# The boundaries of a two-layer latent trunk in a fixed order: pinned tail products, statistics and rows, a Newton iteration spread over the norm, early weight loads

## The chip, the cores and the metric

The kernel runs on one core of a Trainium2 chip. Its time is the device time of one execution in microseconds, the median of several runs; lower is better. The engines that matter here are TensorE (PE in the profile; PEld is its weight load), VectorE (DVE), ScalarE (ACT), GpSimd (POOL) and SyncE (SP), which issues nearly all transfers.

## What is computed

The reference is a trunk of two layers over 256 latent tokens and 256 context tokens, each of 1024 features. Each layer has three sub-layers, each with a norm ahead of it and a gated residual behind it:

```python
def rmsnorm(x, g):
    y = x * lax.rsqrt(jnp.mean(x * x, axis=-1, keepdims=True) + NORM_EPS)
    return y * g
def modulate(h, shift, scale):
    return h * (1 + scale) + shift
def ffn_half_step(h, m, k, g, w_gate, w_up, w_down):
    shift, scale, gate = m[:, :, 3 * k], m[:, :, 3 * k + 1], m[:, :, 3 * k + 2]
    hn = modulate(rmsnorm(h, g), shift, scale)
    return h + 0.5 * gate * swiglu(hn, w_gate, w_up, w_down)
...
for i in range(DEPTH):                       # DEPTH = 2
    m_lat = adaln_params(c, mod_w[i], mod_b[i])       # 9 vectors of 1024
    m_ctx = adaln_params(c_ctx[None, :], mod_w[i], mod_b[i])
    lat, cx = ffn_half_step(lat, m_lat, 0, ...), ffn_half_step(cx, m_ctx, 0, ...)
    # i = 0: latent attention heads and S5 groups; i = 1: Hyena and RG-LRU channels
    lat, cx = lat + m_lat[5] * y_lat, cx + m_ctx[5] * y_ctx
    lat = ffn_half_step(lat, m_lat, 2, ...)
    if not last: cx = ffn_half_step(cx, m_ctx, 2, ...)
return rmsnorm(lat, final_norm)
```

The feed-forward width is 2816. All of it is float32.

## The kernel before

**Layout.** Features lie on the 128 partitions and tokens in the free dimension: a feature tile is 128 x 512, columns 0 to 255 context (`CTX`), 256 to 511 latent (`LAT`). The residual `res` stays in SBUF as eight such tiles.

**Products.** A float32 product is made of three passes (`mm3`, L149 to L151): high part of the weights with the high part of `x` (L149), high with low (L150), low with high (L151). `wload` fetches a block of weights into `raw` (four buffers, SyncE's queue), ScalarE casts it into the high part (L141), and a subtraction gives the low part (L142): on VectorE, but on GpSimd for the second and third block of each norm's front. The split weights `w` have four buffers.

**Sub-layers and boundaries.** The order is ffn(0,0), even mixer, ffn(0,2), ffn(1,0), odd mixer, ffn(1,2) on the latent half alone, final norm. At the end of a sub-layer `down` takes the first five feature tiles with both halves at once, and the last three, the *tail*, half by half: three context tiles (128x256), then three latent ones. `residual` (L394) adds each into `res`; `stat` squares it (L269, ScalarE) and adds it to the half's `acc` (L270). `rstd_stats` sums `acc` over the partitions (two products with one column, L236) and takes 1/sqrt by three Newton iterations on one-column tiles (L241 to L249: `rs_v`, `rs_a`, `rs_y`); `rstd_rows` spreads the result over the partitions by two products (L256). Then comes the *front* of the next sub-layer, `norm_proj`: `norm_tile` makes `nt` (L287, VectorE), the high part of `x` (L292, ScalarE) and the low part (L294, VectorE), and each tile of `x` goes at once into the products of three blocks, eight context tiles first, then eight latent ones. Statistics and rows of the latent half come near the end of the context tiles.

**Order.** A scheduler decides at build time in which order each engine's instructions stand. `high_priority(offset=SOON)` lets a group go ahead of others; `keep` (keep_in_program_order) pins an instruction behind the one pinned before it on its engine. Before, the Newton steps, norm steps, statistics and rows are pinned; the products of tail and front are not.

**Background jobs.** Two kinds of work are cut into steps that `tick` doles out between the products: `mod_job` computes the vectors of `adaln_params` by reductions on VectorE (L215, 128x1024, one for each condition and feature tile), and `s5_prepare` and `hyena_prepare` build the matrices of the mixers. In `s5_chunk` (eight passes) six rounds double a row of angles (L635), and `_wrap` (L451, L452) takes the nearest integer off after each.

**Pools.** SBUF is divided anew for each stage (`phase`). The first use of a new stage's tile waits for all users of the pools that were given back.

## Time and profile before

| | before |
|---|---|
| median of 3 runs | 1827.52 us (1824.61 to 1829.32) |
| span of the profiled execution | 1825.2 us |
| PE busy | 1742.0 us (95%), 9364 products |
| DVE busy | 1307.9 us (72%), 2582 instructions |
| ACT busy | 684.6 us (38%) |
| POOL busy | 37.0 us (2%), 57 instructions |
| chain that ended last | PE 83%, DVE 9%, DMA 3%, ACT 2% |

The busy time of an engine is a mean over stretches of different kind. In the 40 slices of the page PE stands at nine tenths or more nearly everywhere. Lower digits lie in the first slice, in the last and in five between.

### The profile page before, as it was taken

The numbers are of one execution on the slowest core, as the hardware profiler recorded it, in microseconds if no ns is written. First come the engines' busy times: TensorE is split into PE (matmuls) and PEld (weight loads), VectorE is DVE, ScalarE is ACT, GpSimd is POOL, SyncE is SP. The second block draws the span as 40 slices with busy tenths as digits, with TensorE's granted clock in tenths as the row PEclk, the third lists the DMA queues.
The fourth block names the chain that finished last, engine by engine and source line by source line (L and its number), as shares of the span: only waits on it lengthen the run. The fifth ranks groups of instructions, "written<-read, shape, count | busy, mean of one in ns | idle before, by whom it ended". The sixth has DMA issues, their size and how long they took to land.

```text
span 1825.2 us, 24880 instructions
## 1 busy us (share of the span) xinstructions
PE 1742.0 (95%) x9364; PEld 1456.1 (80%) x9364; DVE 1307.9 (72%) x2582; ACT 684.6 (38%) x1082; POOL 37.0 (2%) x57
## 2 busy tenths in 40 slices
PE   5999999997999998999999999999999989789997
PEld 3778777787877787778888888888888888589997
DVE  7999999898578667775666677766653476975555
ACT  4433333333345654222222233222122247554442
POOL 0000000001000000000000010000000000010000
PEclk9999999998998999999999999999999999889998
DMA  8466666652465452664554533554533225236562
GB/s 320 167 213 203 207 205 202 211 193 96 124 187 160 131 170 89 191 208 141 159 184 150 161 116 124 175 174 152 171 116 93 81 81 198 71 130 194 181 190 92
DMA packets 108057, 292.64 MB, mean 160 GB/s; under 512 B 21217, under 2 KB 36449, under 8 KB 107681
## 3 DMA queue, kind: packets, MB, share of 16 engines
q1 hardware_dynamic: 102368, 287.39, 49.2%
q10 hardware_dynamic: 4928, 2.10, 0.6%
q0 software_dynamic: 640, 1.57, 0.3%
q8 instruction: 73, 1.20, 0.3%
q14 instruction: 48, 0.39, 0.1%
HBM read 272.20 MB, written 18.28 MB: 159 GB/s over the span
## 4 chain that ended last, share of the span: by engine, by line
PE 83%; DVE 9%; DMA 3%; ACT 2%; issue 1%; SPq 1%; DVEq 0%; ACTq 0%
PE mm L149 26%; PE mm L150 26%; PE mm L151 26%; DVE w L142 1%; DMA raw<-in_wgu_dram 1%; DVE acc L270 1%; DVE rs_y L249 1%; ACT w L141 1%; DMA x<-d_g 1%; DMA h<-in_modw_dram 1%; DMA x<-d_v 0%; SPq L943 0%; DVE rs_a L247 0%; DVE nt L287 0%; DVE junk L215 0%
## 5 line engine op out<-in xcount | busy, mean ns | idle before, releaser
L150 PE MATMUL mm<-x,w 128*128 128x512 f32 (+1 forms) x1792 | 631.6, 355 | 3.3 <-DVE x L294 3.3
L151 PE MATMUL mm<-x,w 128*128 128x512 f32 (+1 forms) x1792 | 630.1, 354 | 0.0
L149 PE MATMUL mm<-x,w 128*128 128x512 f32 (+1 forms) x1792 | 613.9, 357 | 11.4 <-ACT x L292 9.9
L141 ACT CAST w<-raw 128x1024 fp32r<-128x1024 f32 (+2 forms) x328 | 332.5, 1018 | 532.8 <-issue 267.4
L142 DVE TENSOR_TENSOR w<-raw,w 128x1024 fp32r<-128x1024 f32 (+2 forms) x318 | 376.5, 1187 | 164.0 <-ACT w L141 163.3
L149 PEld LDWEIGHTS mm<-x,w 128*128 128x128 f32 x1792 | 334.9, 192 | 65.8 <-ACT x L292 10.9
L150 PEld LDWEIGHTS mm<-x,w 128*128 128x128 f32 x1792 | 343.4, 192 | 52.2 <-DVE x L294 4.3
L151 PEld LDWEIGHTS mm<-x,w 128*128 128x128 f32 x1792 | 343.1, 192 | 49.3 <-issue 1.8
L215 DVE CUSTOM_DVE_ANT_0 junk<-m,sc 128x1024 f32<-128x1024 f32 x256 | 312.4, 1220 | 2.2
L149 PE MATMUL mm<-h,w 128*128 128x512 f32 (+1 forms) x776 | 270.3, 351 | 0.0
L150 PE MATMUL mm<-h,w 128*128 128x512 f32 (+1 forms) x776 | 270.1, 349 | 0.0
L151 PE MATMUL mm<-h,w 128*128 128x512 f32 (+1 forms) x776 | 269.8, 349 | 0.0
L150 PEld LDWEIGHTS mm<-h,w 128*128 128x128 f32 x776 | 146.2, 188 | 21.2 <-issue 1.4
L149 PEld LDWEIGHTS mm<-h,w 128*128 128x128 f32 x776 | 145.9, 189 | 21.5 <-issue 1.1
L151 PEld LDWEIGHTS mm<-h,w 128*128 128x128 f32 x776 | 146.2, 188 | 20.3 <-issue 0.4
L394 DVE SCALAR_TENSOR_TENSOR res<-mm,mraw,res 128x256 f32<-128x256 f32 x192 | 86.1, 479 | 97.1 <-PE mm L151 96.6
L422 DVE TENSOR_TENSOR h<-h,mm 128x512 f32<-128x512 f32 (+1 forms) x88 | 54.6, 620 | 125.2 <-PE mm L151 108.5
L421 ACT ACTIVATE h<-mm 128x512 f32<-128x512 f32 (+1 forms) x88 | 47.9, 544 | 238.3 <-PE mm L151 238.2
L292 ACT ACTIVATE x<-nt,mraw 128x256 fp32r<-128x256 f32 x88 | 43.0, 506 | 75.3 <-DVE nt L287 75.2
L156 DVE TENSOR_TENSOR h<-h,h 128x512 fp32r<-128x512 f32 (+1 forms) x88 | 54.4, 618 | 0.0
L155 ACT CAST h<-h 128x512 fp32r<-128x512 f32 (+1 forms) x88 | 49.6, 564 | 9.1 <-DVE h L422 9.0
L269 ACT ACTIVATE sq<-res 128x256 f32<-128x256 f32 x84 | 33.3, 413 | 50.4 <-DVE res L394 38.5
(324 smaller groups left out, 1437.1 us busy)
## 6 DMA issues: line engine op xcount, KB each, us to landing
raw<-in_wgu_dram SPq DMA_DIRECT2D x176, 512.0 KB, 3.6
m<-in_modw_dram SPq DMA_DIRECT2D x130, 512.0 KB, 4.2
raw<-in_wd_dram SPq DMA_DIRECT2D x64, 512.0 KB, 3.7
raw<-in_wd_dram SPq DMA_DIRECT2D x32, 384.0 KB, 3.3
raw<-in_od_in_dram SPq DMA_DIRECT2D x20, 512.0 KB, 3.5
h<-in_modw_dram SPq DMA_DIRECT2D x12, 512.0 KB, 10.4
raw<-in_ev_in_dram SPq DMA_DIRECT2D x10, 512.0 KB, 3.8
d_mb<-mbt SPq DMA_DIRECT2D x16, 256.0 KB, 3.0
```

The source lines that it names most:

```text
L141: nc.scalar.copy(w[:, 0, :n], raw[:, :n])
L142: (nc.gpsimd if pool else nc.vector).tensor_sub(w[:, 1, :n], raw[:, :n], w[:, 0, :n])
L149: mm(ps, lhsT=wh, rhs=xh, start=first and i == 0, stop=False)
L150: mm(ps, lhsT=wh, rhs=xl, start=False, stop=False)
L151: r = mm(ps, lhsT=wl, rhs=xh, start=False, stop=last and i == n - 1)
L155: self.nc.scalar.copy(hi, src)
L156: self.nc.vector.tensor_sub(lo, src, hi)
L215: nc.vector.tensor_tensor_reduce(self.junk, w, self.sc[:, v, :], 1.0, 0.0, ALU.mult, ALU.add, raw[:, dt, v : v + 1])
L292: self.last_act = nc.scalar.activation(x[:, 0, c0:c1], y, AF.Identity, bias=b)
L394: self.nc.vector.scalar_tensor_tensor(r, ps[:, c0:c1], gate[:, i, VEC[h] : VEC[h] + 1], r, op0=ALU.mult, op1=ALU.add)
L421: nc.scalar.activation(s[:, 0, lo:hi], pg[:, lo:hi], AF.Silu)
L422: nc.vector.tensor_mul(s[:, 1, lo:hi], s[:, 0, lo:hi], pu[:, lo:hi])
```

## The change

The places where one sub-layer ends and the next begins are written out in a fixed order.
- `down` pins every tail product (`keep=True`). The statistics of the context half stand behind the fifth of the eight feature groups of the first latent tail tile, its row products behind the second latent tail tile. Before the tail, the next sub-layer's first block is loaded (`self.ready`).
- `norm_proj` takes that block, loads the second into tiles of the stage's own pools (`spare`: `x`, `y` or `h`, `g`) and the third into `w`, and pins all front products. The latent half's statistics start at the fourth context tile (`j == 3`), and Newton is given out in four quarters over the tiles 3 to 6; the row products follow ahead of the last context tile. The first two norm steps are not pinned.
- No subtraction of weights is left on GpSimd.
- `phase` makes its pools with `reuse_waits="tile"`: a tile waits only for the users of its own bytes.
- In `mod_job` the five vectors of layer 1 with m > 4 are computed for the latent condition alone (32 reductions fewer).
- In `s5_chunk` `_wrap` is called twice a pass, on wider ranges, instead of six times.

```diff
-            p = self.stage.enter_context(self.tc.tile_pool(name=self.uid(tag), bufs=bufs))
+            p = self.stage.enter_context(self.tc.tile_pool(name=self.uid(tag), bufs=bufs, reuse_waits="tile"))
...
-        (nc.gpsimd if pool else nc.vector).tensor_sub(w[:, 1, :n], raw[:, :n], w[:, 0, :n])
+        if tag is None:
+            w = self.wp.tile([P, 2, 1024], F32R, tag="w", name=self.uid("w"))
+            hi, lo = w[:, 0], w[:, 1]
+        else:
+            hi, lo = (self.slot(tag, [P, 1024], F32R) for _ in range(2))
+        nc.scalar.copy(hi[:, :n], raw[:, :n])
+        nc.vector.tensor_sub(lo[:, :n], raw[:, :n], hi[:, :n])
...
-                for v in range(2):
+                for v in range(1 if l and m > 4 else 2):
...
+        ws = [self.ready, self.wload(srcs[1], D, spare), self.wload(srcs[2], D)] if spare else None
...
+                low[j]()
+                if j == 3:
+                    self.st = self.rstd_steps([self.acc[halves[1]]], self.inv_d)
+                if 3 <= j < 7:
+                    next(self.st[2], None)
             for w, ps in zip(ws, pss):
-                self.mm3(ps[:, h[0] : h[1]], self.wparts(w, KT)[i : i + 1], self.parts(xs[i : i + 1], *h), i == 0, i == KT - 1)
+                self.mm3(ps[:, h[0] : h[1]], self.wparts(w, KT)[i : i + 1], self.parts(xs[i : i + 1], *h), i == 0, i == KT - 1, keep=True)
...
+        ws = [(i, self.wload(blocks(i), n * P), self.pm()) for i in range(KT - tail, KT)]
+        self.ready = self.wload(after, D)
+        for h in halves:
+            for m, (i, w, ps) in enumerate(ws):
+                for j in range(n):
+                    if h is halves[1] and (m, j) == (0, 5):
+                        with self.tc.high_priority(offset=SOON):
+                            st = self.stats(halves[0])
+                    self.mm3(
+                        ps[:, h[0] : h[1]], self.wparts(w, n)[j : j + 1], self.parts(xs[j : j + 1], *h), j == 0, j == n - 1, keep=True
+                    )
+                self.residual(i, ps, gate, h, last)
+                if h is halves[1] and m == 1:
                     with self.tc.high_priority(offset=SOON):
-                        self.rb[h] = self.rstd_rows(*self.stats(h))
+                        self.rb[halves[0]] = self.rstd_rows(*st)
...
-            n, tt = a[:, :, w : 2 * w], tm[:, : 8 * w].rearrange("p (g c) -> p g c", g=8)
-            e.tensor_add(n, a[:, :, :w], tn[:, g8].unsqueeze(2).to_broadcast([P, 8, w]))
-            self._wrap(e, n, tt)
+            e.tensor_add(a[:, :, w : 2 * w], a[:, :, :w], tn[:, g8].unsqueeze(2).to_broadcast([P, 8, w]))
+            if w in (4, 32):
+                x = a[:, :, 1 : 2 * w] if w == 4 else a[:, :, 8 : 2 * w]
+                self._wrap(e, x, tm[:, : 8 * x.shape[-1]].rearrange("p (g c) -> p g c", g=8))
```

**TensorE at the third boundary**, from ffn(0,2) to ffn(1,0). `mm_8848`, `mm_8854` and `mm_8860` are the three tail tiles, `acc_8674` is the context half's sum, `ps_8945` holds its statistics and rows, `x_9052` is the first tile of the norm, and `mm_9075` to `mm_9077` are the front's three blocks. Before:

```order
L149 MATMUL mm_8854<-h_8346,w_8851 128x256
L236 MATMUL ps_8945<-inv_d,acc_8674 128x1 x2
L150 MATMUL mm_8854<-h_8346,w_8851 128x256
...
L151 MATMUL mm_8860<-h_8632,w_8857 128x256
L256 MATMUL ps_8945<-ident,rs_y_8949 128x128 x2
L149 MATMUL mm_9075<-x_9052,w_9062 128x256
L149 MATMUL mm_9076<-x_9052,w_9067 128x256
L149 MATMUL mm_9077<-x_9052,w_9072 128x256
L150 MATMUL mm_9075<-x_9052,w_9062 128x256
```

The same place of the change; the tail tiles are now `mm_8786`, `mm_8792` and `mm_8798`, the second block lies in the spare tiles `h_8997` and `h_8998`, the third in `w_9003`:

```order
L155 MATMUL mm_8786<-h_8354,w_8783 128x256 x3
L253 MATMUL ps_8903<-inv_d,acc_8612 128x1 x2
L155 MATMUL mm_8786<-h_8428,w_8783 128x256 x3
...
L155 MATMUL mm_8792<-h_8570,w_8789 128x256 x3
L278 MATMUL ps_8903<-ident,rs_y_8907 128x128 x2
L155 MATMUL mm_8798<-h_8067,w_8795 128x256 x3
...
L155 MATMUL mm_9014<-x_9006,w_8801 128x256 x3
L155 MATMUL mm_9015<-x_9006,h_8997 128x256 x2
L155 MATMUL mm_9015<-x_9006,h_8998 128x256
L155 MATMUL mm_9016<-x_9006,w_9003 128x256 x3
L155 MATMUL mm_9014<-x_9007,w_8801 128x256 x3
```

The statistics moved from the second latent tail tile up into the first, the row products from behind the last latent tail tile to ahead of it (24 products follow them), and a tile of the front takes all its nine products in a row, block by block. The latent half's statistics now stand behind the front's third context tile, before behind the sixth.

**VectorE at the same place.** `w_9322` is the fourth block's low part, `w_9062` to `w_9072` the front's three. Before:

```order
L241 TENSOR_SCALAR rs_v_8948<-ps_8945 128x2
L270 TENSOR_TENSOR acc_8677<-acc_8677,sq_8993 128x256
L242 TENSOR_SCALAR rs_y_8949<-rs_v_8948 128x2
L243 TENSOR_SCALAR rs_v_8948<-rs_v_8948 128x2
...
L270 TENSOR_TENSOR acc_8677<-acc_8677,sq_9021 128x256
L394 SCALAR_TENSOR_TENSOR res<-mm_8860,mraw_8_6518,res 128x256
L287 SCALAR_TENSOR_TENSOR nt_9078<-res,mraw_1_7323,ps_8945 128x256
L287 SCALAR_TENSOR_TENSOR nt_9081<-res,mraw_1_7323,ps_8945 128x256
L142 TENSOR_TENSOR w_9322<-raw_9320,w_9322 128x1024
```

With the change; `w_9003` is the third block's low part, `w_9261` and `w_9303` are the fourth's and fifth's:

```order
L267 SCALAR_TENSOR_TENSOR rs_a_8908<-rs_y_8907,rs_v_8906 128x1
L149 TENSOR_TENSOR w_9003<-raw_9001,w_9003 128x1024
L267 SCALAR_TENSOR_TENSOR rs_a_8908<-rs_y_8907,rs_v_8906 128x1
...
L309 SCALAR_TENSOR_TENSOR nt_9020<-res,mraw_1_7261,ps_8903 128x256
L149 TENSOR_TENSOR w_9261<-raw_9259,w_9261 128x1024
L292 TENSOR_TENSOR acc_8615<-acc_8615,sq_8962 128x256
L316 SCALAR_TENSOR_TENSOR x_9006<-nt_9017,mraw_0_6885,x_9006 128x256
...
L429 SCALAR_TENSOR_TENSOR res<-mm_8798,mraw_8_6456,res 128x256
L149 TENSOR_TENSOR w_9303<-raw_9301,w_9303 128x1024
L316 SCALAR_TENSOR_TENSOR x_9008<-nt_9033,mraw_0_6885,x_9008 128x256
...
L309 SCALAR_TENSOR_TENSOR nt_9134<-res,mraw_1_7261,ps_9063 128x256
L316 SCALAR_TENSOR_TENSOR x_9013<-nt_9115,mraw_0_6885,x_9013 128x256
```

The third block's subtraction stands inside the context half's Newton steps, those of two more blocks among the first norm steps, and the first latent norm step (`nt_9134`, which reads the latent rows in `ps_9063`) ahead of the low part of the last context tile (`x_9013`).

**VectorE at the first boundary**, from ffn(0,0) to the even mixer. Before, reductions of the background job (L215, an ISA row each) and S5's angles (L635, L452) stand among the Newton steps:

```order
L635 TENSOR_TENSOR et_2602<-et_2602,sb_19_162 128x8x32
L247 SCALAR_TENSOR_TENSOR rs_a_3782<-rs_y_3781,rs_v_3780 128x1 x2
L270 TENSOR_TENSOR acc_3521<-acc_3521,sq_3853 128x256
L451 TENSOR_SCALAR tm_2385<-et_2602 128x256
L249 SCALAR_TENSOR_TENSOR rs_y_3781<-rs_a_3782,rs_y_3781 128x1 x2
L452 TENSOR_TENSOR et_2602<-et_2602,tm_2385 128x8x32
L215 ISA junk_625,mraw_7_2401<-m_2627,sc_624 128x1024
```

With the change the same Newton steps follow each other:

```order
L269 SCALAR_TENSOR_TENSOR rs_y_3737<-rs_a_3738,rs_y_3737 128x1
L267 SCALAR_TENSOR_TENSOR rs_a_3738<-rs_y_3737,rs_v_3736 128x1 x2
L269 SCALAR_TENSOR_TENSOR rs_y_3737<-rs_a_3738,rs_y_3737 128x1 x2
L267 SCALAR_TENSOR_TENSOR rs_a_3738<-rs_y_3737,rs_v_3736 128x1
L149 TENSOR_TENSOR w_3871<-raw_3869,w_3871 128x1024
```

All reductions and angles of this stage now stand ahead of the tail. The fifth boundary, from the odd mixer to ffn(1,2), keeps its order.

## Rows read from the trace of the kernel before

**Rows 1.** Windows: length, busy us (instructions) by engine, granted clock, DMA share, GB/s.

```profile
65.00:430.00 365.00, 361.61 (x1752) 291.36 (x1750) 335.28 (x679) 130.38 (x205) 5.76 (x11) 1.00 0.63 201
```

**Rows 2.** Timeline of PE, third boundary: start, us, instruction, [idle before it].

```profile
1063.58 0.29 PE L149 MATMUL mm<-h,w 128*128 128x256 f32 x1
...
1099.29 0.85 PE L149 MATMUL mm<-x,w 128*128 128x256 f32 x4 [0.32 <-ACT x L292]
```

**Rows 3.** Windows over the four boundaries, columns PE, PEld, DVE, ACT, POOL.

```profile
407.81:450.60 42.79, 32.61 (x250) 30.73 (x248) 36.95 (x106) 14.61 (x27) 4.83 (x2) 0.84 0.37 120
669.14:706.57 37.43, 32.22 (x235) 30.76 (x233) 24.78 (x71) 11.53 (x21) 4.74 (x2) 0.91 0.22 72
1063.58:1099.29 35.71, 31.09 (x233) 29.99 (x232) 23.46 (x68) 11.53 (x21) 4.75 (x2) 0.90 0.23 74
1443.92:1480.41 36.49, 31.47 (x233) 30.45 (x231) 23.45 (x66) 11.54 (x21) 4.75 (x2) 0.91 0.18 58
```

**Rows 4.** Timeline of PE inside the third boundary.

```profile
1076.30 0.50 PE L236 MATMUL ps<-inv_d,acc 128*128 128x1 f32 x4
1076.66 0.36 PE L150 MATMUL mm<-h,w 128*128 128x256 f32 x1
...
1081.14 0.28 PE L151 MATMUL mm<-h,w 128*128 128x256 f32 x1
...
1097.47 0.71 PE L256 MATMUL ps<-ident,rs_y 128*128 128x128 f32 x4 [0.50 <-DVE rs_y L249]
1097.99 0.38 PE L150 MATMUL mm<-x,w 128*128 128x256 f32 x1
```

**Rows 5.** Timeline of PE, second boundary: filter products.

```profile
703.24 0.64 PE L990 MATMUL ps<-y 33*64 33x256 f32 x2
```

**Rows 6.** Timeline of PE, first boundary: a group of S5 products.

```profile
408.98 0.43 PE L614 MATMUL ps<-gs,bank 128*32 128x128 f32 x8
```

**Rows 7.** Lines of PE, third boundary: busy us, mean ns, idle before and its releasers.

```profile
L149 PE MATMUL mm<-x,w 128*128 128x256 f32 x24 | 5.4, 343 | 1.1 <-ACT x L292 1.1
L256 PE MATMUL ps<-ident,rs_y 128*128 128x128 f32 x8 | 1.4, 301 | 2.5 <-DVE rs_y L249 2.5
```

**Rows 8.** Timeline of DVE, third boundary.

```profile
1076.92 2.24 DVE L270 TENSOR_TENSOR acc<-acc,sq 128x256 f32<-128x256 f32 x1
...
1079.74 2.43 DVE L249 SCALAR_TENSOR_TENSOR rs_y<-rs_a,rs_y 128x1 f32<-128x1 f32 x2
...
1084.94 1.22 DVE L142 TENSOR_TENSOR w<-raw,w 128x1024 fp32r<-128x1024 f32 x1
...
1086.80 0.48 DVE L287 SCALAR_TENSOR_TENSOR nt<-res,mraw,ps 128x256 f32<-128x256 f32 x1
1087.19 0.48 DVE L294 SCALAR_TENSOR_TENSOR x<-nt,mraw,x 128x256 fp32r<-128x256 f32 x1
...
1095.48 0.16 DVE L241 TENSOR_SCALAR rs_v<-ps 128x2 f32<-128x2 f32 x1 [3.87 <-PE ps L236]
...
1098.22 0.48 DVE L287 SCALAR_TENSOR_TENSOR nt<-res,mraw,ps 128x256 f32<-128x256 f32 x1 [0.28 <-PE ps L256]
```

**Rows 9.** Windows with TensorE's granted clock, columns as in rows 1.

```profile
622.00:626.00 4.00, 2.79 (x23) 1.87 (x24) 0.00 (x0) 3.58 (x6) 0.75 (x1) 1.00 0.65 168
1088.00:1090.00 2.00, 2.00 (x11) 2.00 (x11) 2.00 (x7) 1.34 (x3) 0.00 (x0) 0.50 0.49 199
```

**Rows 10.** Lines of DVE from 409.5 to 440 us, first boundary.

```profile
L215 DVE CUSTOM_DVE_ANT_0 junk<-m,sc 128x1024 f32<-128x1024 f32 x9 | 10.9, 1216 | 0.0
L635 DVE TENSOR_TENSOR et<-et,sb 128x16 f32<-128x16 f32 (+4 forms) x5 | 3.5, 696 | 0.0
```

**Rows 11.** Timeline of ACT, third boundary: a cast.

```profile
1075.30 1.05 ACT L141 CAST w<-raw 128x1024 fp32r<-128x1024 f32 x1 [1.88 <-PE mm L151]
```

**Rows 12.** Timeline of DVE, second boundary: first of the filter steps.

```profile
703.92 0.54 DVE L991 TENSOR_SCALAR y<-ps,y 64x256 f32<-64x256 f32 x1 [0.37 <-PE ps L990]
```

**Rows 13.** Source line 452, the subtraction of `_wrap`: ns min/median/max, times, forms.

```profile
L452 DVE TENSOR_TENSOR et<-et,tm x48: 165/206/427, 98.1 to 429.7; 128x8 f32<-128x8 f32 x8, 128x16 f32<-128x16 f32 x8, 128x32 f32<-128x32 f32 x8, 128x64 f32<-128x64 f32 x8
```

More of the change, by code (lines that the diff above doesn't have):

```diff
@@ L37 @@
 NPASS = 8
+EVEN, ODD = (7, 8, 4), (12, 13, 14)
 GPP = 4
@@ L229, in rstd_stats, with rstd_steps @@
     def rstd_stats(self, accs, inv):
+        rb, y, steps = self.rstd_steps(accs, inv)
+        for _ in steps:
+            pass
+        return rb, y
+    def rstd_steps(self, accs, inv):
         cols = [a[:, j : j + P] for a in accs for j in range(0, a.shape[-1], P)]
@@ L321, in norm_proj @@
             return xs, pss
-        ws = [self.wload(s, D, i > 0) for i, s in enumerate(srcs)]
         pss = [self.pm() for _ in srcs]
+        first = lambda: self.tc.high_priority(offset=SOON)
         if len(halves) == 1:
-            self.rb[halves[0]] = self.rstd_rows(*self.stats(halves[0]))
-        todo = [(n, h, i) for n, h in enumerate(halves) for i in range(KT)]
+            ws = [self.wload(s, D) for s in srcs]
+            h = halves[0]
+            self.rb[h] = self.rstd_rows(*self.stats(h))
+            tile = lambda i: self.norm_tile(l, k, i, h, xs[i])
+            with first():
+                low = tile(0)
+            for i in range(KT):
+                with first():
+                    nxt = tile(i + 1) if i + 1 < KT else None
+                    low()
+                low = nxt
+                for w, ps in zip(ws, pss):
+                    self.mm3(ps[:, h[0] : h[1]], self.wparts(w, KT)[i : i + 1], self.parts(xs[i : i + 1], *h), i == 0, i == KT - 1)
+            return xs, pss
+        todo = [(h, i) for h in halves for i in range(KT)]
         low = {}
@@ L362, in wparts, with down @@
     def wparts(self, w, n, m=P, o=0):
-        return [(w[:, 0, o + i * m : o + (i + 1) * m], w[:, 1, o + i * m : o + (i + 1) * m]) for i in range(n)]
-    def down(self, blocks, xs, gate, halves, last, n):
+        return [(w[0][:, o + i * m : o + (i + 1) * m], w[1][:, o + i * m : o + (i + 1) * m]) for i in range(n)]
+    def down(self, blocks, xs, gate, halves, last, n, after=None):
         lo, hi = halves[0][0], halves[-1][1]
@@ L377, in down @@
                 self.tick()
-        if tail:
-            ws = [(i, self.wload(blocks(i), n * P), self.pm()) for i in range(KT - tail, KT)]
-            for h in halves:
-                for i, w, ps in ws:
-                    self.mm3(ps[:, h[0] : h[1]], self.wparts(w, n), self.parts(xs, *h))
-                    self.residual(i, ps, gate, h, last)
-                if h is not halves[-1]:
+        if not tail:
+            return
+        ws = [(i, self.wload(blocks(i), n * P), self.pm()) for i in range(KT - tail, KT)]
[11 more added lines that the diff above has]
+                if h is halves[1] and m == 1:
                     with self.tc.high_priority(offset=SOON):
-                        self.rb[h] = self.rstd_rows(*self.stats(h))
+                        self.rb[halves[0]] = self.rstd_rows(*st)
     def stats(self, h):
@@ L398, in residual, with blocks, ffn @@
             self.stat(i, h)
-    def ffn(self, l, k, halves, lead=None):
+    def blocks(self, idx, n=3):
+        return [self.t["wgu"][idx, b // 2, b % 2] for b in range(n)]
+    def ffn(self, l, k, halves, after=None, spare=None, lead=None):
         nc, t = self.nc, self.t
@@ L405, in ffn @@
         wgu = t["wgu"][idx]
-        blocks = [wgu[f, g] for f in range(2) for g in range(2)]
-        xs, pss = self.norm_proj(l, k, halves, blocks if lead else blocks[:3], lead)
+        xs, pss = self.norm_proj(l, k, halves, self.blocks(idx, 4 if lead else 3), lead, spare if len(halves) > 1 else None)
         if lead is not None:
@@ L427, in ffn @@
             gate = self.need(l, 3 * k + 2)
-            self.down(lambda i: t["wd"][idx, i][:, f0 * P : f1 * P], hid, gate, halves, f1 == NF, f1 - f0)
+            self.down(lambda i: t["wd"][idx, i][:, f0 * P : f1 * P], hid, gate, halves, f1 == NF, f1 - f0, after)
     def proj(self, name, blk, xs, c0, c1):
@@ L659, in even_mixer @@
         blk = t["ev_in"]
-        xs, pss = self.norm_proj(0, 1, both, [blk[i] for i in (7, 8, 4)])
+        xs, pss = self.norm_proj(0, 1, both, [blk[i] for i in EVEN], spare="x")
         qn = self.const([P, 5], "qkvn", t["qkvn"])
@@ L1068, in odd_mixer @@
         both = [CTX, LAT]
-        xs, pss = self.norm_proj(1, 1, both, [t["od_in"][12 + i] for i in range(3)])
+        xs, pss = self.norm_proj(1, 1, both, [t["od_in"][i] for i in ODD], spare="g")
         pss.append(self.proj("od_in", 15, xs, 0, T2))
```

91 lines of the change are left out of this document (41 added, 50 removed).

## The prediction, made before the changed kernel ran

> **What bounds the kernel now.** I read the windows first. In the long feed-forward stretches TensorE never stops: in 65 to 430 us it is busy 361.6 of 365.0 us, although VectorE, the next engine, is busy 335.3 [rows 1]. No cut in another engine's work can shorten such a stretch. What is left to win lies where one sub-layer ends and the next begins, because there the norm stands between the last products and the first ones. So I measured those places in the timeline of TensorE: from the first product of the tail (three feature tiles taken half by half, 128x256) to the first latent product of the next sub-layer's front [rows 2]. Between them stand always the same 144 tail products and 72 context products of the front, two groups of statistics products and two of row products. Four such boundaries exist. Windows laid from the first to the last of these products give 42.8, 37.4, 35.7 and 36.5 us, in which TensorE is idle for 10.2, 5.2, 4.6 and 5.0 and is granted a mean clock of 0.84 to 0.91 [rows 3].
>
> The least that they can last comes from the timeline. 38 products from 1076.66 to 1081.14 give 4.48 / 37 = 0.121 us each; a group of statistics takes 1076.66 - 1076.30 = 0.36, a group of row products 1097.99 - 1097.47 = 0.52 [rows 4]. 216 x 0.121 + 2 x 0.36 + 2 x 0.52 = 27.9 us. So the third boundary loses 35.7 - 27.9 = 7.8 us and the fourth 8.6. In the second, two filter products stand inside: 0.64 less the 0.16 by which a product's end lies over the next one [rows 4, 5]. 37.4 - 27.9 - 0.5 = 9.0. In the first, two groups of S5 products of 0.43 stand inside [rows 6]: 42.8 - 27.9 - 0.9 = 14.0. Together **39.4 us**, 2.2% of the time; the kernel can't win more here.
>
> Why they are lost is seen in the third. TensorE waits 2.5 us in all for the row products' input `rs_y`, and 1.1 us for `x` from ScalarE [rows 7]. The reader is to see what held `rs_y` up: an addition to `acc` took 2.24 us and a pair of one-column steps 2.43 us, though a norm step of the shape of the first takes 0.48, and the whole Newton of the latent half, fifteen small steps, 1097.47 - 1095.48 = 2.0 [rows 4, 8]. Both lie on GpSimd's two subtractions, 4.75 us together [rows 3]: VectorE stood still while GpSimd ran. [...] In the first boundary there is twice the idle time, since nine reductions of the background job (1.22 us each, 10.9 us in all) share VectorE with the norm there [rows 10].
>
> **The change, part by part.**
>
> *GpSimd's subtractions go to VectorE.* Eight of them, 1.22 us each there [rows 8]. At the four boundaries the second block's weights now load ahead of the tail into spare buffers, where VectorE has room; that one costs nothing (without this cover, 1.22 us more in the walk below). The third block's subtraction stands inside the Newton steps and is counted below. The stalls of some 2 us go.
>
> *The pinned order.* I walk the third boundary in microseconds from the tail's first product, along the order shown above. VectorE issues one 128x256 step every 0.39 us (1086.80, 1087.19) [rows 8]; a cast on ScalarE takes 1.05 [rows 11]. Context tail: 72 x 0.121 = 8.7. Fifteen latent products, 10.5. By then the last context square is just added: residual, square and addition, priced like a step's 0.48 [rows 8] and begun at 8.9, end at 10.3. Statistics to 10.9, nine products to 12.0, the second latent tile to 14.9. VectorE starts Newton at 11.1. Alone it takes 2.0 us. But the third block's subtraction stands inside it, and its cast can start only when the first tail tile's weights are done, at 12.0 + 0.2; cast to 13.3, subtraction to 14.5, one addition and the last four small steps to 15.2. TensorE waits **0.3**, then the rows to 15.7 and the third latent tile to 18.6. The first norm step starts 0.75 us after the row products (1098.22 - 1097.47) [rows 4, 8], at 16.0. Then on VectorE, in order: two norm steps, the fourth block's subtraction, an addition, `x` 0 low (done 18.8), norm, `x` 1 low (19.6), norm, the last residual, the fifth block's subtraction, `x` 2 low (done 21.9). TensorE takes tiles 0 and 1 from 18.6 to 20.8 (9 x 0.121 = 1.09 each) and waits **1.0** for tile 2. It waits **0.2** for the last latent square, then gives the statistics at 23.0. From there each tile costs VectorE two steps and one quarter of Newton's 2.0, 0.79 + 0.5 = 1.29 against TensorE's 1.09: it waits **0.5, 0.2, 0.2** for tiles 4 to 6. Tile 7's low part stands behind the first latent norm step, which needs the new rows: **1.0**. Waits 3.4 us, first latent product at 27.9 + 3.4 = **31.3** instead of 35.7.
>
> So an order pinned this way still leaves 3.4 us a boundary: VectorE becomes what the front waits for, in short waits. I take the same 3.4 for the first and fourth, and 4.4 for the second, where three filter steps (0.54 for the first [rows 12], I put 1.0 for all) stand ahead of the first latent norm step. Gain: 14.0 - 3.4, 9.0 - 4.4, 7.8 - 3.4, 8.6 - 3.4 = 10.6 + 4.6 + 4.4 + 5.2 = **24.8 us**. It includes that no wait is long enough to bring the clock down. Bounds: no waits at all, 39.4 (nothing better can be read from the rows); the clock down as now, about 3.2 us a boundary (7.8 less 4.6 of idle time), 24.8 - 12.8 = 12.0.
>
> On the clock the rows stand first: in 622 to 626 TensorE was idle for 30% of the time and kept 1.00 [rows 9]. [...]
>
> *The first boundary's background work* now stands ahead of the tail. 10.9 us of reductions and 3.5 of S5 steps [rows 10] are pushed into a stretch in which VectorE is idle for 365 - 335.3 = 29.7 us [rows 1]. In the same edit the wraps of the S5 angles shrink from twelve steps to four per pass: each of eight passes loses eight steps of about 0.2 us [rows 13], less what the wider remaining ones cost more; I put 1.2 a pass. Net at most 5 us more in 29.7 idle; I take zero, and 5 us if the idle time lies in the wrong places.
>
> *Pools that wait tile by tile* let the spare blocks and `x` start before the old stage is done. That is cover for the parts above and has no price of its own. *Thirty-two fewer reductions* (the context column of five unused vectors; 32 x 1.22 = 39 us of VectorE) lie beside products that never wait: nothing. *The fifth boundary* (Hyena to the last feed-forward) keeps its order. Its two blocked additions become two subtractions of 1.22, still ahead of the last statistics: nothing, within 1 us.
>
> *Sum.* The profiled span is 1825.2 us, and the median of the runs 1827.5, 2.3 more. 1825.2 - 24.8 = 1800.4 for the span, and **1802.7** for the median.
>
> **The rivals.**
> *A: the clock falls all the same*, since short waits come back every microsecond or two in the fronts. [...] For it: now the level falls at every one of these places. Against it: 622 to 626. 1827.5 - 12.0 = 1815.5.
> *B: VectorE is overfull before the first tail.* TensorE then waits in 380 to 408. At most the 14.4 us that were moved, of which 9.6 would be won back by the shorter wraps: 1807 to 1808.
> *C: the waits nearly vanish*, because the scheduler's fillers (the fourth and fifth blocks' subtractions) come earlier on the chip than in my walk. 1 us a boundary: gain 39.4 - 5 = 34, 1793.
> *D: slower.* All products of the front are pinned tile by tile through three blocks, so the third block's load now holds the whole front. Its transfer stands on SyncE's queue behind loads that wait for a reduction. If it lands late, all four boundaries wait by that much. By the walk it must have landed by 12.2; each microsecond after 14 costs 4 us. From 14 + 24.8 / 4 = 20.2 on the kernel is slower, at 24 by 15 us: 1842. Against it: the buffer that it takes is free long before the tail, since only four loads share them.
> *E: nothing changes*, when the walk's VectorE is late everywhere by as much as now (a lateness of 6 us a boundary from D's cause or from several small ones): 1827.
>
> **How the numbers follow.** The forecast 60%, A 12%, B 8%, C 10%, D 5%, E 5%. Predicted is the likeliest, 1802.7. Its own range is 1798 to 1808 (waits of 2.2 to 4.7 us a boundary). Reaching to C below and to A above, past their middles, gives 1791 to 1817 and leaves out D, E and a third of A and C, under 2 in 10. A measurement of this kernel tells 0.3%, 5.5 us, from no change. Faster by more: forecast, A, B and C, 90%, of which I give back 5 for what I have not thought of: 0.85. Same: E and a part of that, 0.08. Slower: D and the rest, 0.07.
>
> **What would show it.** Boundaries of about 31 us in the timeline, where 36 to 43 stand now; `acc` and `rs_y` at their own durations; granted clock 1.00 through all four; short waits of products for `x` low, the longest at tiles 2 and 7. The forecast is wrong if the clock still falls (A), if a product before 408 waits for a weight's subtraction (B), or if the front's first products wait for the third block's cast (D).

## The result, and the profile after

The changed kernel takes **1795.55 us** (median of 4 runs, 1795.14 to 1796.36) against 1826.53 (4 runs, 1824.61 to 1829.32): a ratio of 0.983, 95% interval 0.9817 to 0.9843. The forecast was 1802.7 with a range of 1791 to 1817. The profiled execution's span went from 1825.2 to 1793.4 us, 31.8 less. Its page begins so; the columns are busy us, share of the span and number of instructions:

```profile
span 1793.4 us, 24725 instructions
PE 1727.7 (96%) x9364; PEld 1444.7 (81%) x9364; DVE 1252.9 (70%) x2464; ACT 684.1 (38%) x1082; POOL 13.2 (1%) x47
```

Windows over the four boundaries, from the first tail product to the first latent product of the front as in [rows 3], with the same columns:

```profile
408.12:438.91 30.79, 29.11 (x233) 28.02 (x232) 22.98 (x73) 11.68 (x22) 0.00 (x0) 1.00 0.24 80
656.45:687.85 31.40, 29.71 (x235) 28.22 (x234) 25.17 (x77) 11.87 (x22) 0.00 (x0) 1.00 0.36 119
1045.08:1075.97 30.89, 29.20 (x233) 28.06 (x232) 23.63 (x73) 11.88 (x22) 0.00 (x0) 1.00 0.29 97
1419.15:1450.06 30.91, 29.23 (x233) 28.11 (x232) 22.84 (x70) 11.68 (x22) 0.00 (x0) 1.00 0.21 69
```

The reader is to see three things against [rows 3]. The lengths are 30.8, 31.4, 30.9 and 30.9 us where 42.8, 37.4, 35.7 and 36.5 stood: 12.0 + 6.0 + 4.8 + 5.6 = 28.4 of the 31.8 us. GpSimd's column is empty. The granted clock is 1.00 throughout.

The timeline of TensorE in the third boundary. The first row is the first tail product; of the front the rows of the second block's three products are shown, one row for each of the eight context tiles, so that the distance from row to row is what a tile takes:

```profile
1045.08 10.61 PE L155 MATMUL mm<-h,w 128*128 128x256 f32 x87
...
1063.88 0.51 PE L155 MATMUL mm<-x,h 128*128 128x256 f32 x3
...
1064.94 0.52 PE L155 MATMUL mm<-x,h 128*128 128x256 f32 x3
...
1066.64 0.50 PE L155 MATMUL mm<-x,w 128*128 128x256 f32 x2 [0.71 <-DVE x L316]
1066.98 0.52 PE L155 MATMUL mm<-x,h 128*128 128x256 f32 x3
...
1068.67 0.52 PE L155 MATMUL mm<-x,h 128*128 128x256 f32 x3
...
1070.15 0.52 PE L155 MATMUL mm<-x,h 128*128 128x256 f32 x3
...
1071.39 0.52 PE L155 MATMUL mm<-x,h 128*128 128x256 f32 x3
...
1072.63 0.52 PE L155 MATMUL mm<-x,h 128*128 128x256 f32 x3
...
1074.91 0.50 PE L155 MATMUL mm<-x,w 128*128 128x256 f32 x2 [0.85 <-DVE x L316]
1075.25 0.52 PE L155 MATMUL mm<-x,h 128*128 128x256 f32 x3
```

A tile without a wait takes 1064.94 - 1063.88 = 1.06 us. The others take 2.04, 1.69, 1.48, 1.24, 1.24 and 2.62. Less the 1.06, and less 0.4 for the statistics ahead of tile 3 and 0.36 for the rows ahead of tile 7, that is a wait of 1.0 at tile 2, 0.2 at tile 3, 0.4 at tile 4, 0.2 at 5 and 6, 1.2 at tile 7: **3.2 us** a boundary. The idle time printed in brackets shows only 0.71 and 0.85 of it, since a short wait is hidden under the modelled end of the product before. Waits of this size are read from starts.

VectorE at the same place, rows that carry these waits:

```profile
1059.67 0.42 DVE L292 TENSOR_TENSOR acc<-acc,sq 128x256 f32<-128x256 f32 x1
...
1064.97 1.22 DVE L149 TENSOR_TENSOR w<-raw,w 128x1024 fp32r<-128x1024 f32 x1
1066.11 0.48 DVE L316 SCALAR_TENSOR_TENSOR x<-nt,mraw,x 128x256 fp32r<-128x256 f32 x1
...
1073.98 0.48 DVE L309 SCALAR_TENSOR_TENSOR nt<-res,mraw,ps 128x256 f32<-128x256 f32 x1 [1.29 <-PE ps L278]
1074.38 0.48 DVE L316 SCALAR_TENSOR_TENSOR x<-nt,mraw,x 128x256 fp32r<-128x256 f32 x1
```

The addition to `acc` takes 0.42 us where one of 2.24 stood [rows 8]. The low part of tile 2 stands behind the fifth block's subtraction (1064.97), that of tile 7 behind the first latent norm step, which waited 1.29 us for the rows.

Outside the boundaries 3.4 us are left. About 1.5 lie between the third and the fourth, where TensorE is busy without a break in both kernels (see the last section); the rest is spread over the other stretches in pieces of 1 us or less.

### The profile page after: what moved, and what is told of

Its sections match the earlier page's. It is cut to its first block, busy times and chain, and to the rows that moved or that the text cites. A ratio compares the mean times of both kernels' runs of the same rounds, so it can differ in the third digit from the quotient of the medians.

```text
span 1793.4 us, 24725 instructions
## 1 busy us (share of the span) xinstructions
PE 1727.7 (96%) x9364; PEld 1444.7 (81%) x9364; DVE 1252.9 (70%) x2464; ACT 684.1 (38%) x1082; POOL 13.2 (1%) x47
## 4 chain that ended last, share of the span: by engine, by line
PE 87%; DVE 7%; DMA 2%; ACT 1%; issue 1%; SPq 1%; DVEq 0%; ACTq 0%
PE mm L158 25%; PE mm L160 25%; PE mm L159 25%; PE mm L155 6%; DVE w L149 1%; DMA h<-in_modw_dram 1%; PE mm L1148 1%; SPq L981 1%; DVE nt L309 1%; DMA x<-d_g 1%; DVE x L316 1%; DMA x<-d_v 0%; PE ps L278 0%; PE ps L631 0%; PE ps L1059 0%
## 5 line engine op out<-in xcount | busy, mean ns | idle before, releaser
L159 PE MATMUL mm<-x,w 128*128 128x512 f32 (+1 forms) x1600 | 575.1, 360 | 0.0
L160 PE MATMUL mm<-x,w 128*128 128x512 f32 (+1 forms) x1600 | 574.5, 360 | 0.0
L158 PE MATMUL mm<-x,w 128*128 128x512 f32 (+1 forms) x1600 | 569.4, 361 | 4.5 <-ACT x L314 3.3
L148 ACT CAST w<-raw 128x1024 fp32r<-128x1024 f32 (+2 forms) x324 | 328.5, 1018 | 527.7 <-issue 254.1
L149 DVE TENSOR_TENSOR w<-raw,w 128x1024 fp32r<-128x1024 f32 (+2 forms) x324 | 384.0, 1187 | 191.7 <-ACT w L148 190.8
L158 PEld LDWEIGHTS mm<-x,w 128*128 128x128 f32 x1600 | 300.9, 189 | 55.9 <-ACT x L314 3.9
L159 PEld LDWEIGHTS mm<-x,w 128*128 128x128 f32 x1600 | 301.8, 189 | 48.9 <-issue 2.0
L160 PEld LDWEIGHTS mm<-x,w 128*128 128x128 f32 x1600 | 301.8, 189 | 48.7 <-issue 1.2
L225 DVE CUSTOM_DVE_ANT_0 junk<-m,sc 128x1024 f32<-128x1024 f32 x224 | 273.3, 1220 | 1.8 <-DMA m<-in_modw_dram 0.2
L158 PE MATMUL mm<-h,w 128*128 128x512 f32 (+1 forms) x632 | 229.2, 367 | 0.0
L160 PE MATMUL mm<-h,w 128*128 128x512 f32 (+1 forms) x632 | 228.4, 364 | 0.0
L159 PE MATMUL mm<-h,w 128*128 128x512 f32 (+1 forms) x632 | 228.3, 363 | 0.0
L159 PEld LDWEIGHTS mm<-h,w 128*128 128x128 f32 x632 | 119.1, 188 | 20.6 <-issue 1.0
L158 PEld LDWEIGHTS mm<-h,w 128*128 128x128 f32 x632 | 118.6, 188 | 21.0 <-issue 1.1
L160 PEld LDWEIGHTS mm<-h,w 128*128 128x128 f32 x632 | 118.9, 188 | 20.5 <-issue 0.6
L155 PE MATMUL mm<-x,w 128*128 128x256 f32 x384 | 66.1, 289 | 6.7 <-DVE x L316 6.2
L155 PEld LDWEIGHTS mm<-x,w 128*128 128x128 f32 x384 | 53.9, 188 | 11.6 <-DVE x L316 9.2
```

What stands on the lines that cost most here:

```text
L148: nc.scalar.copy(hi[:, :n], raw[:, :n])
L149: nc.vector.tensor_sub(lo[:, :n], raw[:, :n], hi[:, :n])
L155: mm = lambda *a, **k: self.keep(self.nc.tensor.matmul(*a, **k))
L158: mm(ps, lhsT=wh, rhs=xh, start=first and i == 0, stop=False)
L159: mm(ps, lhsT=wh, rhs=xl, start=False, stop=False)
L160: r = mm(ps, lhsT=wl, rhs=xh, start=False, stop=last and i == n - 1)
```

## Experiments

**Theory 1** is the prediction's: GpSimd's subtractions held VectorE up, TensorE waited for rows and `x`, and its clock fell; the pinned order puts products over these waits. **Rival 2**: early loads and pools that wait tile by tile bring the gain. **Rival 3**: the lighter VectorE does. Theory 4 came up later and is told there. Each kernel was timed beside the kernel before on the same chip; all ratios are against that.

| kernel | median us | ratio (95%) | boundary read: us, clock |
|---|---|---|---|
| changed kernel | 1795.55 | 0.983 (0.9817 to 0.9843) | third 30.89, 1.00 |
| b_sub_dve | 1816.51 | 0.9941 (0.9925 to 0.9958) | third 34.86, 0.90; fourth 32.45, 1.00 |
| b_reuse | 1827.19 | 1.0002 (0.9993 to 1.0011) | third 36.38, 0.91 |
| a_nopin | 1813.04 | 0.9928 (0.9913 to 0.9943) | third 34.48, 0.95 |
| a_bg | 1808.68 | 0.9902 (0.9885 to 0.9919) | first 41.22, 0.88; third 30.88, 1.00 |
| a_sub_pool | 1802.37 | 0.9858 (0.9842 to 0.9875) | third 31.94, 1.00 |
| a_newton_once | 1803.64 | 0.9869 (0.9854 to 0.9884) | third 33.57, 0.95 |
| a_noearly | 1798.64 | 0.9842 (0.9827 to 0.9857) | third 30.92, 1.00 |
| a_best | 1790.59 | 0.9798 (0.9783 to 0.9812) | third 28.75, 1.00 |
| a_wrap6 | 1809.02 | 0.9898 (0.9874 to 0.9922) | first 41.18, 0.88 |
| a_red | 1797.29 | 0.9833 (0.9814 to 0.9853) | third 30.89, 1.00 |
| b_wrap2 | 1820.74 | 0.9966 (0.9950 to 0.9982) | first 35.08, 0.95 |
| a_tailpin | 1803.03 | 0.9867 (0.9847 to 0.9887) | third 31.78, 1.00; fourth 32.94, 0.95 |

**b_sub_dve: the kernel before, no subtraction on GpSimd**

```diff
-        ws = [self.wload(s, D, i > 0) for i, s in enumerate(srcs)]
+        ws = [self.wload(s, D) for i, s in enumerate(srcs)]
```

> The kernel before, with one edit: the subtractions of the second and third block run on VectorE instead of GpSimd. Theory 1 (GpSimd held VectorE up, and the idle time that followed brought TensorE's clock down): additions to acc and steps of rs_y take their own 0.2 to 0.5 us, but two subtractions of 1.22 us now stand among the Newton steps, and the tail's order is as before. TensorE waits about 1.5 us less at each boundary: 6 us less in all if the clock still falls (about 1820), up to 19 less if it stays up (1808). Rival 2 (early loads and pools that wait tile by tile bring the gain) and rival 3 (the lighter VectorE brings it): 1826, no change beyond 3 us.

It won 10.3 us, inside the expected 6 to 19. Windows of the third and fourth boundary, and a stretch of the third:

```profile
1058.34:1093.20 34.86, 31.08 (x233) 30.26 (x232) 21.84 (x70) 11.48 (x21) 0.00 (x0) 0.90 0.21 76
1437.84:1470.29 32.45, 28.68 (x233) 27.77 (x232) 21.82 (x68) 11.50 (x21) 0.00 (x0) 1.00 0.19 66
1081.00:1086.00 5.00, 5.00 (x27) 5.00 (x26) 4.04 (x11) 2.79 (x6) 0.00 (x0) 0.55 0.04 16
```

Timeline of TensorE at the first front product, third and fourth boundary:

```profile
1079.85 1.01 PE L149 MATMUL mm<-x,w 128*128 128x256 f32 x3 [2.17 <-ACT x L292]
...
1459.20 0.62 PE L149 MATMUL mm<-x,w 128*128 128x256 f32 x3 [2.17 <-ACT x L292]
```

In both, TensorE waits 0.8 us for the rows and 2.17 for `x`, yet the clock stayed at 1.00 in the fourth and fell to 0.55 in a stretch of the third. The difference, 34.86 - 32.45 = 2.4 us, comes with the clock.

**b_reuse: the kernel before, pools that wait tile by tile**

```diff
-            p = self.stage.enter_context(self.tc.tile_pool(name=self.uid(tag), bufs=bufs))
+            p = self.stage.enter_context(self.tc.tile_pool(name=self.uid(tag), bufs=bufs, reuse_waits="tile"))
```

> The kernel before, with one edit: the stage pools wait tile by tile. Theory 1: nothing that TensorE waits for at the boundaries hangs on it; 1826, within 3 us. Rival 2 (cover): at least half of the 31 us, 1811 or less, with shorter boundaries. Rival 3: 1826.

Nothing, within 0.1%. Rival 2's first half falls.

**a_noearly: the changed kernel, blocks loaded when the front begins**

```diff
-        ws = [self.ready, self.wload(srcs[1], D, spare), self.wload(srcs[2], D)] if spare else None
...
+        ws = [self.wload(s, D) for s in srcs] if spare else None
...
-        self.ready = self.wload(after, D)
+        self.late = after
```

> The changed kernel without early loads: first, second and third block are loaded when the front begins, into the four shared weight buffers, as before. Theory 1: the third block's buffer is that of the second latent tail tile, free 2.9 us later than now, its cast and its subtraction (1.22) come among the first norm steps, and TensorE waits about 1 to 2 us for it at the first front tile: 4 to 8 in all, 1800 to 1804. Rival 2 (early loads are what the gain comes from): the waits of before come back, 15 us or more, with a fall of the clock.

All boundaries are as long as with early loads (30.92 against 30.89 in the third), and the intervals of the ratios overlap. Rival 2 falls altogether; theory 1's 4 to 8 us were too much. The casts of the blocks come at the same places behind the tail's tiles, only each block takes the place of the next one, and the third is ready before TensorE reaches it.

**a_sub_pool: the changed kernel, third block's subtraction on GpSimd**

```diff
-        nc.vector.tensor_sub(lo[:, :n], raw[:, :n], hi[:, :n])
+        (nc.gpsimd if pool else nc.vector).tensor_sub(lo[:, :n], raw[:, :n], hi[:, :n])
...
-        ws = [self.ready, self.wload(srcs[1], D, spare), self.wload(srcs[2], D)] if spare else None
+        ws = [self.ready, self.wload(srcs[1], D, spare), self.wload(srcs[2], D, pool=True)] if spare else None
```

> The changed kernel, but the third block's subtraction runs on GpSimd at the four boundaries, as before. Theory 1: it lies in the context half's Newton steps; a step with two SBUF operands stands still for up to 2.4 us, the row products come 1.2 to 1.7 us later, and TensorE waits that long: 5 to 7 us in all (1801 to 1803), up to 18 if the clock falls (1813). Rival 2 (early loads and pools bring the gain): 1796, since VectorE is relieved of 1.22 us a boundary and loads are unchanged; rival 3 would even expect 1793.

6.8 us lost, as expected. Timelines of VectorE, GpSimd and TensorE in its third boundary:

```profile
1062.44 2.35 DVE L269 SCALAR_TENSOR_TENSOR rs_y<-rs_a,rs_y 128x1 f32<-128x1 f32 x1
...
1062.38 2.39 POOL L149 TENSOR_TENSOR w<-raw,w 128x1024 fp32r<-128x1024 f32 x1 [387.35 <-ACT w L148]
...
1064.84 0.89 PE L278 MATMUL ps<-ident,rs_y 128*128 128x128 f32 x4 [0.75 <-DVE rs_y L269]
```

A step on one column, otherwise 0.15 us, takes as long as the whole subtraction; VectorE is relieved of 1.22 us and the kernel is slower all the same. The boundaries account for 0.9 to 1.05 us each (31.94 against 30.89 in the third), 4.0 in all, at a granted clock of 1.00; the rest lies outside them (see the last section).

**a_nopin and a_tailpin: without the pins, and with those on the tail alone**

```diff
-                self.mm3(ps[:, h[0] : h[1]], self.wparts(w, KT)[i : i + 1], self.parts(xs[i : i + 1], *h), i == 0, i == KT - 1, keep=True)
+                self.mm3(ps[:, h[0] : h[1]], self.wparts(w, KT)[i : i + 1], self.parts(xs[i : i + 1], *h), i == 0, i == KT - 1)
...
-                        ps[:, h[0] : h[1]], self.wparts(w, n)[j : j + 1], self.parts(xs[j : j + 1], *h), j == 0, j == n - 1, keep=True
+                        ps[:, h[0] : h[1]], self.wparts(w, n)[j : j + 1], self.parts(xs[j : j + 1], *h), j == 0, j == n - 1
```

(a_tailpin makes only the first of the two edits.)

> The changed kernel without the pins on the tail's and the front's products; the rest (early loads, no GpSimd, spread Newton, lighter background) stays. The context half's row products then stand behind all tail products again, as before. Theory 1: from there TensorE waits for the first norm tile, about 0.75 + 1.3 us after the rows, where the pinned order had 24 products to lie over it; tiles then come every 0.79 us against 1.09, so that the waits of 0.7 and 0.14 us in the first context tiles vanish. Net 0.5 to 1.5 us a boundary, 2 to 6 in all: 1798 to 1802; up to 12 more if the clock falls in that wait. Rivals 2 and 3: 1796, since loads and VectorE's load are unchanged.

17.5 us lost, at the upper end, with a falling clock: 0.95 in all four boundaries, which hold 13.9 of the loss. Timeline of TensorE and a window in its third boundary:

```profile
1073.69 0.71 PE L278 MATMUL ps<-ident,rs_y 128*128 128x128 f32 x4 [0.78 <-DVE rs_y L269]
1076.57 0.39 PE L158 MATMUL mm<-x,w 128*128 128x256 f32 x1 [2.17 <-ACT x L314]
...
1079.00:1084.00 5.00, 5.00 (x37) 4.90 (x36) 2.23 (x12) 1.02 (x2) 0.00 (x0) 0.83 0.00 0
```

The waits are those of b_sub_dve to the hundredth: without pins the rows stand behind the whole tail, and nothing lies over the first norm tile. So, by what its absence costs, the pinned order is the largest single part of the gain.

> The changed kernel with the pins on the tail's products kept and those on the front's taken off. Theory 1 as mended by the run without any pins (the gain of the pins is that 24 tail products lie over the rows and the first norm steps): the context rows stand ahead of the last tail tile still, and little is lost: 1796 to 1799. Rival (it is the front's order, tile by tile through three blocks, that counts): 1805 or more, near the 1813 without pins.

It lies between the two. The pins on the tail give back 10 of the 17.5 us; those on the front are worth the other 7.5, of which about 4.7 lie in the four boundaries. Timeline of TensorE in its third boundary:

```profile
1072.08 0.50 PE L253 MATMUL ps<-inv_d,acc 128*128 128x1 f32 x4
1074.02 0.39 PE L159 MATMUL mm<-x,w 128*128 128x256 f32 x1 [1.44 <-DVE x L316]
```

Left alone, the scheduler put the latent statistics behind the first three products of tile 4, one tile later. The first Newton steps are pinned on VectorE ahead of tile 4's low part; so tile 4 waits for statistics that stand behind its own first products.

**a_newton_once: all of the latent Newton at one place**

```diff
-                if 3 <= j < 7:
-                    next(self.st[2], None)
+                    for _ in self.st[2]:
+                        pass
```

> The changed kernel, but all four quarters of the latent half's Newton stand together behind the fourth context tile instead of over the tiles 3 to 6. Theory 1: the low part of tile 4 comes some 1.3 us later and TensorE waits about 1.2 us there; later tiles come every 0.79 us against 1.09, which gives nothing back at tile 7, whose low part still stands behind the latent rows; since these rows are ready earlier, part of the 0.85 us there may go. Net 0.4 to 1.2 us a boundary, 2 to 5 in all: 1797 to 1801. Against it: only VectorE's sum up to tile 7 counts, then 1796 within 1.

8.1 us lost, about 6.5 of them in the four boundaries. Timeline of TensorE and the two windows around it in the third boundary, then the same wait in the fourth and the window of the whole fourth boundary:

```profile
1075.00 0.78 PE L155 MATMUL mm<-x,w 128*128 128x256 f32 x2 [1.64 <-DVE x L316]
...
1070.00:1075.00 5.00, 3.02 (x22) 2.71 (x22) 4.20 (x22) 0.93 (x2) 0.00 (x0) 1.00 0.30 107
1075.00:1080.00 5.00, 5.00 (x29) 5.00 (x30) 1.52 (x4) 1.11 (x3) 0.00 (x0) 0.66 0.00 0
...
1451.76 0.51 PE L155 MATMUL mm<-x,w 128*128 128x256 f32 x2 [1.64 <-DVE x L316]
...
1425.53:1457.58 32.05, 28.85 (x234) 27.95 (x232) 22.92 (x71) 11.68 (x22) 0.00 (x0) 1.00 0.19 67
```

The wait at tile 4 is there in all four boundaries (1.64 to 1.66 us, about 1.2 expected). What was not expected is the clock, which fell to 0.66 behind it in the third: 33.57 against 30.89 us. In the other three it stayed at 1.00, and they last 31.93, 32.99 and 32.05 us.

**a_bg, a_wrap6, a_red, b_wrap2: the background work**

a_bg undoes both lines, a_wrap6 the wraps alone, a_red the reductions alone; b_wrap2 is the kernel before with the new wraps.

```diff
-                for v in range(1 if l and m > 4 else 2):
+                for v in range(2):
...
-            e.tensor_add(a[:, :, w : 2 * w], a[:, :, :w], tn[:, g8].unsqueeze(2).to_broadcast([P, 8, w]))
-            if w in (4, 32):
-                x = a[:, :, 1 : 2 * w] if w == 4 else a[:, :, 8 : 2 * w]
-                self._wrap(e, x, tm[:, : 8 * x.shape[-1]].rearrange("p (g c) -> p g c", g=8))
+            n, tt = a[:, :, w : 2 * w], tm[:, : 8 * w].rearrange("p (g c) -> p g c", g=8)
+            e.tensor_add(n, a[:, :, :w], tn[:, g8].unsqueeze(2).to_broadcast([P, 8, w]))
+            self._wrap(e, n, tt)
```

> The changed kernel with the background work of before: 32 reductions more (39 us of VectorE) and the wraps in six rounds a pass. Theory 1: all of it lies beside products that do not wait, and the first boundary is clear of it by the order; 1796 within 2 us, all four boundaries as in the changed kernel. Rival 3 (the lighter VectorE brings the gain): at least 10 us back, in the first boundary or in waits for weights ahead of it, 1806 or more.

Theory 1 was wrong here: 13 us came back in the median. In the profiled execution, the slowest of the four, it is 18.1: 10.4 in the first boundary, none in the other three (31.49, 30.90 and 30.91 us), 4.4 in the even mixer behind the first (not explained), and 2.2 in the last feed-forward (see the last section). From it theory 4: ahead of the first tail VectorE lacks usable room, and the shorter wraps make it.

> The changed kernel with one half of the old background work: the wraps in six rounds a pass again, the 32 reductions stay out. With both halves the time was 1808.7, and its first boundary had ten reductions and the last angles among the norm's steps. Theory 4 (VectorE lacks room ahead of the first tail; the shorter wraps make it): 1806 to 1810, the first boundary longer by some 10 us, the others as in the changed kernel. Rival (the 32 reductions, later on, are what counted): 1796.

> The changed kernel with the other half: the 32 reductions (39 us of VectorE in the feed-forwards of layer boundaries two to four) are back, the wraps stay short. Theory 4: 1796 within 2, all boundaries as in the changed kernel. Rival: 1803 or more, with waits of products for weights.

> The kernel before with the short wraps alone. Theory 4: the reductions and angles leave the first boundary without any pinned order, which then lasts about what the others do, 36 to 37 us instead of 42.8: 6 to 7 us less, 1820 to 1821. Rival (it takes the new order to move them): 1826.

All three came as theory 4 has it: 1809.0, 1797.3 and 1820.7. Windows of the first boundary in a_wrap6 and b_wrap2, the stretch ahead of it in a_wrap6, and the costliest line of VectorE in a_wrap6's first boundary:

```profile
408.56:449.74 41.18, 34.01 (x250) 32.36 (x248) 37.23 (x111) 15.85 (x29) 0.00 (x0) 0.88 0.41 135
65.00:408.56 343.56, 343.56 (x1590) 273.70 (x1591) 314.86 (x626) 123.78 (x192) 1.01 (x9) 1.00 0.62 202
...
409.16:444.24 35.08, 30.12 (x234) 29.10 (x232) 23.39 (x66) 11.54 (x21) 4.75 (x2) 0.95 0.17 60
...
L225 DVE CUSTOM_DVE_ANT_0 junk<-m,sc 128x1024 f32<-128x1024 f32 x10 | 12.2, 1217 | 0.0
```

With the old wraps ten reductions stay in the pinned boundary although VectorE is idle for 343.56 - 314.86 = 28.7 us ahead of it. With the new ones they leave even the unpinned boundary of before, which shrinks from 42.8 to 35.1.

**a_best: the two waits that were left**

`pin` is `keep` for the first two loads behind the front, those of the fourth and fifth block.

```diff
+        pin(nc.vector.tensor_sub(lo[:, :n], raw[:, :n], hi[:, :n]))
...
-                if j == KT:
-                    self.rb[h] = self.rstd_rows(*self.st[:2])
...
+                if j == KT - 1:
+                    low[j]()
                 front(j + 1)
-                low[j]()
+                if j != KT - 1:
+                    low[j]()
...
-                if 3 <= j < 7:
-                    next(self.st[2], None)
+                if 3 <= j < 6:
+                    for _ in range(2 if j == 4 else 1):
+                        next(self.st[2], None)
+                if j == 6:
+                    self.rb[halves[1]] = self.rstd_rows(*self.st[:2])
```

> The changed kernel with three edits at each boundary, aimed at the two waits that are left: the subtractions of the fourth and fifth block are pinned behind the norm steps; the latent rows stand one tile earlier (Newton's quarters over the tiles 3 to 5); tile 7's low part stands ahead of the first latent norm step. Theory 1 (VectorE's queue is what the front waits for): the waits of 0.70 us at tile 2 and 0.85 at tile 7 go, 4 to 6 us in all, 1790 to 1792. Against it: the waits move to tiles 5 and 6, where Newton is packed closer, or to the fourth block's products; then 1795 within 1.5.

It takes 1790.59 us, 5.0 less than the changed kernel and the fastest of all; the intervals of the two ratios do not touch. Window of its third boundary and the only long wait in it:

```profile
1042.07:1070.82 28.75, 28.24 (x234) 27.72 (x233) 21.65 (x71) 11.76 (x22) 0.00 (x0) 1.00 0.18 64
...
1067.16 0.50 PE L158 MATMUL mm<-x,w 128*128 128x256 f32 x2 [0.36 <-DVE x L319]
```

28.75 us is 0.9 above the floor of 27.9. The waits of 1.0 and 1.2 us are gone; what remains is short, by starts 0.6 at tile 5, 0.4 at tile 4 and 0.1 elsewhere.

## Why the prediction was right, point by point

**The place and the floor.** The gain was put at the four boundaries, with 39.4 us to win there. 28.4 of the 31.8 us came from there, and a_best shows that the floor can nearly be reached.

**The walk.** It gave 31.3 us for the third boundary; 30.89 came. Its waits were 0.3 for the rows, 1.0 at tile 2, 0.2 for the last square, 0.5, 0.2 and 0.2 at tiles 4 to 6, 1.0 at tile 7. By starts they are 0, 1.0, 0.2, 0.4, 0.2, 0.2 and 1.2, each at the place that was named, for the cause that was named. That a_best takes away the waits at tiles 2 and 7 by moving the steps of VectorE that stood ahead of their low parts shows the causes of these two.

**What was mis-sized.** The first boundary was put at 27.9 + 0.9 + 3.4 = 32.2, with the S5 products inside; they moved out, and 30.8 came. The second was given 1.0 for the filter steps and 0.5 for their products, 32.8; 31.4 came. These two terms are 2.8 of the 3.6 us by which the boundaries beat the forecast; the third and the fourth, at 30.9 where 31.3 was put, are the rest. The other 3.4 us lie outside the boundaries and had no term.

**GpSimd.** Shown by a_sub_pool and b_sub_dve: a one-column step takes 2.35 us beside a subtraction of 2.39, and otherwise 0.15. a_sub_pool has one such step in each boundary, 2.33 to 2.35 us, and in b_sub_dve none is left. The kernel before has also a step with one operand that was held, in the first boundary beside a subtraction of 2.45 us (424.93), and in the third one that was not:

```profile
425.06 2.34 DVE L243 TENSOR_SCALAR rs_v<-rs_v 128x2 f32<-128x2 f32 x1
...
1076.84 0.16 DVE L241 TENSOR_SCALAR rs_v<-ps 128x2 f32<-128x2 f32 x1 [1.05 <-PE ps L236]
...
1076.48 2.39 POOL L142 TENSOR_TENSOR w<-raw,w 128x1024 fp32r<-128x1024 f32 x1 [388.84 <-ACT w L141]
```

Elsewhere the first of these steps takes 0.17 us. What decides which steps are held is not shown.

**The clock (rival A).** It stayed at 1.00 in all four boundaries with waits of up to 1.2 us in the fronts, as the row of 622 to 626 had suggested [rows 9]; so it did in the four of a_red and the four of a_noearly, which are as long. That waits this short bring the clock down by coming back every microsecond or two, the ground of rival A, is shown by no run. Behind the 2.17 us of a_nopin the clock fell in all four boundaries (0.95 in each), behind the 1.64 of a_newton_once in one of four (0.95 in the third). So the rival's price was real where waits are longer; what makes the clock fall at one place and not at another with the same wait stays open. That the whole 3.2 us a boundary in the bound of 12.0 is the clock's was the author's estimate and is shown by no run: in the third boundary against the fourth, with waits of the same size, the fall cost 2.4 us in b_sub_dve and 33.57 - 32.05 = 1.5 in a_newton_once, and in a_tailpin, where it came in the fourth, 32.94 - 31.78 = 1.2.

**The first boundary's background (rival B).** The forecast took zero, by 29.7 us of idle VectorE and the shorter wraps. The size was right and the reason only half: the idle time as a sum was no cover, since a_wrap6 leaves 12.2 us of reductions behind with 28.7 us idle. It was the short wraps that moved them: without them the first boundary is 10.4 us longer and the median 13 higher, near the 14.4 of rival B before its deduction. How they do it is argued, not shown. With them VectorE is busy for 318.2 of 343.1 us ahead of the tail, more than without (314.9 of 343.6); the order is set at build time, and no run tells room on the chip from the scheduler's placement.

**Costed at nothing.** Pools (b_reuse) and the 32 reductions (a_red) are worth nothing that stands clear of the noise, as put. The early load was called a cover worth 1.22 us a boundary; a_noearly shows that it covers nothing here. The fifth boundary is 0.6 us shorter (6.3 and 5.7 us from the last product ahead of the statistics to the row products), within the 1 us allowed.

**The sum.** The parts do not add up singly: without GpSimd 10.3, with the short wraps 5.6, without the pins 17.5 lost, without the wraps 13 lost. An unpinned order (a_nopin, clock 0.95) and a spilled background (a_wrap6, 0.88) each suffice to make TensorE wait and the clock fall; the one GpSimd subtraction of a_sub_pool makes it wait at a clock of 1.00. So taking one away while another stays wins less: a_nopin has both no GpSimd and the short wraps and is 13.7 us below the kernel before, where each of the two alone won 10.3 and 5.6.

## What to carry to other kernels

Where a saturated engine loses time at the seams (28.4 of the 31.8 us won lay in the four boundaries here), walk one seam in order on the engine that feeds it, and put products that need nothing from the seam over its latency; pins on both engines have to agree, or a step pinned on one waits for something that slid back on the other (1.44 us in a_tailpin). A sum of idle time is no cover (a_wrap6 had 28.7 us of it ahead of the first boundary and 12.2 us of reductions inside): look where the last background steps land. Read short waits from the starts of instructions, not from the idle time that a profile prints.
